# Routing up to the slots ahead of the experts, the data-dependent branch behind them, and the first weight splits on VectorE: one decoder layer on one core

## The chip, the core and the metric

The kernel runs on one core of a Trainium2 chip. The core has five engines with an instruction stream each: TensorE (PE, with the loading of its weights shown apart as PEld), VectorE (DVE), ScalarE (ACT), GpSimd (POOL) and SyncE (SP), and 16 DMA engines that serve the queues of SP and POOL. An engine works its own stream in the order in which it is written and waits on semaphores for the others. The metric is the device time of one execution in microseconds (us). Lower is better.

## The reference

One layer of a decoder for 576 tokens: 512 of a prompt and 64 of a sample (8 sequences of 8). Everything is fp32, with a model width of 1024.

```
proj   = rmsnorm(x) @ w_in                  # 1024 x 5632
y_a    = differential attention(...)        # prompt: causal; sample: a paged cache of 4096
y_r    = HGRN2 gated linear recurrence(...)
merged = sigmoid(gate_a)*(y_a @ w_branch_a) + sigmoid(gate_r)*(y_r @ w_branch_r)
x      = x + merged @ w_out
h      = rmsnorm(x)
group  = top 1 of 4 (h @ w_rg + b);  experts = top 2 of the 4 in that group (h @ w_re + b)
x      = x + sum of 2 of  w * (silu(h @ w_gate[e]) * (h @ w_up[e])) @ w_down[e]     # 16 experts, width 256
x      = x + sigmoid(rmsnorm(x) @ w_ple_gate) * (p @ w_ple)                          # per-layer input
y      = rmsnorm(x)
```

## The kernel before

**Precision.** Products run in fp32r. A weight arrives as a raw fp32 tile and is taken apart in two parts, `hi` (a cast on ACT) and `lo` (raw minus hi, a subtraction on DVE or POOL), and a product is three products of parts.

**Lanes.** The program is written by lanes, Python generators that a small scheduler (`run_lanes`) interleaves while the kernel is built: it keeps an estimate of each engine's clock and takes, of the lanes whose event is set and whose buffers are free, the one of the best priority. What comes out is one fixed stream per engine. All instructions are issued through one helper, so nearly every row of the trace has its line, L209 (L207 after the change); places are told by the tiles' names. Buffers are pools of slots that lanes take and give back.

**Stages.** Input projection, attention and recurrence, the branches and the output projection (`out_second`, products into `acc`, `sc`, `aux`), with the router's logits of each of the five tiles of tokens behind them (`lane_route`; it also stores the normed rows h to memory, `hf_d<-F`). Then comes `lane_dispatch`, a chain of small operations, mostly DVE's, on all tokens at once. It finds each token's group and two experts (`oh`, as bf16 `mb`), counts places with five small products (`aux<-mb,cbf`), and gathers with one-hot products (`rhs`, `am`) the **slots**: for each expert the tokens of its tile of 128 rows. Behind the slots it works out what the later stages need: the number of tiles beyond one per expert (`cnt`, `nov`, `ovb`, `ge`, `ovx`), the slots of those further tiles (`r`, `aux<-r,am`), the place of each token's two results (`rows`) and their weights (`wt`).

**The gap.** Between the last product of the output projection and the first of the experts, PE has only the small products of the dispatch and those of the per-layer input (`ple_mul`, `in<-mr,rp` and `sc<-mr,rp`). Meanwhile the first NG=5 pieces of the experts' weights are split (`lane_msplit`: hi on ACT, lo on POOL), and POOL gathers the rows of the first tiles (`X<-hf_d,slots`).

**The branch.** Before the experts stands `further()`: seven nested `If`s on the number of tiles beyond the 17 that are always worked. With this data none is taken, but every engine has to load the number and jump past the bodies. Its code is there because other data could need it.

```
for j in range(1, MAXOV):
    si.enter_context(tc.If(nov > j))
```

**Experts.** `lane_moe` works 17 tiles: 16 experts, and one further tile. A tile takes 6 pieces of weights of 512 KB (`mload` to slots `mr`, `mro`, `H`; `wsplit` to `mw`, `mwo`), the gathered rows `X` turned on PE (`sc<-constb,X`) and split (`xs`), four groups of products `in<-mw,xs`, the activation `hd`, its turn `sc<-constb,hd`, its split `hs`, and the second product `aux<-mw,hs` / `acc<-mw,hs`, copied to `Yo` and stored (`y_d<-Yo`).

**Tail.** `lane_tail` does the last three `ple_mul`, gathers each token's two results (`mr<-y_d,rows`), adds them (`H<-mr,wt,H`), turns the rows (`sc<-constb,H`), and does the per-layer gate's products and the last norm.

Of the kernel before, what the change touches and what calls it, by code (L numbers as in the profile page):

```python
# [27 lines left out]
H = 4  # L28
# [14 lines left out]
def _consts():  # L43
    """Tables that depend on the shapes alone."""
# [61 lines left out]
PT = ("X", "Xo", "mro")  # L106
NPE = 2
PEV = 9
NMW = 10
NY = 3  # L110
YT = "Yo",
MPACE = 98, 1
HYS = 4, 7
NMX = 0
NX = 2
# [3 lines left out]
PLO = []  # L119
# [19 lines left out]
# the weights' chunks in the order of their use  # L139
# [45 lines left out]
class Engine:  # L185
    """Passes instructions on and keeps an estimate of the engine's clock, by which the lanes are interleaved."""
# [62 lines left out]
class Kern:  # L249
# [16 lines left out]
    # ------------------------------------------------ lanes  # L266
# [39 lines left out]
    def pick(self, *tags, n=1):  # L306
        """Which of several tags has n slots free: one that ends in o is for the further tiles until they are through."""
        def f():
            for t in tags:
                if (t[-1] == "o" if self.inner else t[-1] != "o" or self.fev.t is not None):  # L310
                    if self.used.get(t, 0) + n <= self.cap.get(t, 0) - (0 if self.gapev.t is None else self.mres if t == "mr" else self.hres if t == "H" else 0):
                        return t
            return None
        return f
# [12 lines left out]
    def pool(self, st, name, tags, **kw):  # L327
        """A pool with a number of slots per tag, counted as the lanes take and free them."""
# [26 lines left out]
    def aside(self, f):  # L355
        """Runs f without making the lane wait for what it issues; returns the time it ends."""
# [9 lines left out]
    def rstd(self, ss, n, shape):  # L366
        """(ss / n + EPS) ** -0.5 by Newton's steps from the exponent's estimate."""
# [23 lines left out]
    # ---------------------------------------------------------------- start  # L391
# [19 lines left out]
    def setup_rest(self):  # L411
        nc, a = self.nc, self.a
        # lambda, on every partition
# [12 lines left out]
        # 1 for the first map's rows, -lambda for the second's  # L426
# [5 lines left out]
        # lower bound of the forget gate: f = fa + fb * tanh(z / 2)  # L432
# [22 lines left out]
    def lane_start(self):  # L455
        """x * g_mix in two parts, and the norm's factor per token along the free dimension."""
# [128 lines left out]
    def in_proj(self, i):  # L585
        """One tile of 128 columns of the input projection, for all tokens, with the norm's factor."""
# [68 lines left out]
    def lane_gates(self):  # L655
        """The branches' gates, back from memory."""
# [12 lines left out]
    def to_tok(self, z, tok, tail):  # L669
        """[128, 576] to the token-major [128, 4, 128] and [64, 128]."""  # L670
# [11 lines left out]
    def rope(self, x, c0, c1, sh):  # L682
        """Rotates x ([128, ...] with the positions c0..c1 last) in place."""
# [58 lines left out]
    def lane_attn(self):  # L742
        """Scores and weights of the prompt's attention, by head and block of queries."""
# [38 lines left out]
    def lane_mid(self, waits, st):  # L782
        """When the first phase's lanes are through, their space goes to the next phase's inputs."""
# [13 lines left out]
    # ------------------------------------------------ sample: the new tokens  # L797
# [35 lines left out]
    # ------------------------------------------------ sample: the paged cache  # L833
# [18 lines left out]
    def lane_scores(self):  # L852
        """Scores of 8 pages at a time by (head, page of a pair, token, map), their maxima, weights and sums."""
# [164 lines left out]
    # ---------------------------------------------------------------- branches, output projection  # L1018
# [14 lines left out]
    def branches(self):  # L1033
# [4 lines left out]
        for b in (1, 0):  # L1038
            for m in range(8):
# [21 lines left out]
                if b == 0:  # L1061
# [3 lines left out]
                    def merge():  # L1065
                        nc.gpsimd.tensor_tensor(g, g, gr, op=ALU.add)
# [9 lines left out]
    def rows_setup(self):  # L1076
        """Constants and weights of the routing."""
# [31 lines left out]
    def lane_route(self, i):  # L1109
        """The router's logits of a tile of tokens; its rows with the norm's weights, and behind them what belongs to the norm itself."""  # L1110
        nc = self.nc
        t0, n = TOK[i]
        for j in range(2):
# [11 lines left out]
            def store():  # L1125
                nc.gpsimd.tensor_tensor(hg[:n], xs, self.grow[0][:n, j * 512:j * 512 + 512], op=ALU.mult)
# [40 lines left out]
    # ---------------------------------------------------------------- routing  # L1167
# [3 lines left out]
    # ---------------------------------------------------------------- experts  # L1171
# [16 lines left out]
    def lane_msplit(self, keys):  # L1188
        """The first tiles' weights, while the routing is under way."""
        yield self.gapev  # L1190
        for key in keys:
            yield from self.wsplit(key, True)

    def lane_mx(self, tiles):
        """The tokens' rows of each tile."""
# [3 lines left out]
        for tl in tiles:  # L1199
            if tl == NE:  # L1200
                yield self.slev2
            w = self.pick("X", "Xo")
            yield w
            tag = self.xt[tl] = w()
            x = self.tl(tag, [128, D + 2])
# [1007 lines left out]
```

## Time and profile before

| | before |
|---|---|
| device time, median of 3 runs | 1026.29 us |
| the three runs | 1024.25, 1030.06, 1026.29 us |
| span of the profiled execution | 1028.9 us |
| PE / PEld busy | 957.8 us (93%) / 766.8 us (75%) |
| DVE busy | 675.4 us (66%) |
| ACT busy | 433.4 us (42%) |
| POOL busy | 344.0 us (33%) |

For the profiled execution the trace gives its span, first to last instruction on the core; that is the time against which the rows below add up. It lies among the three runs, 2.6 us above their median. Times inside the span count from its start: the projections, attention and recurrence take the first 727 us, the gap runs from there to some 767, the experts to 944 and the tail to the end. Busy shares are means over all of it.

### The profile page before, as it was taken

The numbers are of one execution on the slowest core, as the hardware profiler recorded it, in microseconds if no ns is written. First come the engines' busy times: TensorE is split into PE (matmuls) and PEld (weight loads), VectorE is DVE, ScalarE is ACT, GpSimd is POOL, SyncE is SP. The second block draws the span as 40 slices with busy tenths as digits, with TensorE's granted clock in tenths as the row PEclk, the third lists the DMA queues.
The fourth block names the chain that finished last, engine by engine and source line by source line (L and its number), as shares of the span: only waits on it lengthen the run. The fifth ranks groups of instructions, "written<-read, shape, count | busy, mean of one in ns | idle before, by whom it ended". The sixth has DMA issues, their size and how long they took to land. (4 is left out here: it accounts for less than half of the span.)

```text
span 1028.9 us, 20982 instructions
## 1 busy us (share of the span) xinstructions
PE 957.8 (93%) x8129; PEld 766.8 (75%) x8129; DVE 675.4 (66%) x1701; ACT 433.4 (42%) x875; POOL 344.0 (33%) x370
## 2 busy tenths in 40 slices
PE   6999999999999999999999989989639999998995
PEld 5986787877877878778878879868427777775683
DVE  6554555567866774864764465433778999996775
ACT  5143544353342323123222232232228888886442
POOL 3125545454455453543463111332340110101200
PEclk9999999999999999999999989999869999998998
DMA  7549989998989898897997437854149999993511
GB/s 235 206 154 406 367 304 341 313 299 287 335 306 344 311 333 284 297 348 240 332 342 289 139 106 264 291 195 179 46 158 326 393 413 411 412 413 136 186 42 51
DMA packets 93066, 278.67 MB, mean 271 GB/s; under 512 B 10288, under 2 KB 15168, under 8 KB 92960
## 3 DMA queue, kind: packets, MB, share of 16 engines
q0 software_dynamic: 42880, 155.28, 42.5%
q1 hardware_dynamic: 48496, 118.73, 31.7%
q10 hardware_dynamic: 1584, 3.24, 0.8%
q8 instruction: 67, 1.10, 0.4%
q14 instruction: 39, 0.32, 0.1%
HBM read 251.95 MB, written 25.27 MB: 269 GB/s over the span
## 5 line engine op out<-in xcount | busy, mean ns | idle before, releaser
L209 PE MATMUL in<-H,hi 128*128 128x288 f32 x1592 | 357.0, 315 | 14.1 <-ACT hi L209 5.9
L209 PEld LDWEIGHTS in<-H,hi 128*128 128x128 f32 x1592 | 258.9, 193 | 52.1 <-issue 31.3
L209 PE MATMUL in<-H,lo 128*128 128x288 f32 x796 | 239.1, 300 | 0.5 <-DVE lo L209 0.5
L209 POOL DMA_INDIRECT V<-in_vc,idxv x128 | 127.8, 998 | 192.1 <-PE acc L209 172.7
L209 POOL DMA_INDIRECT K<-in_kc,idxk x128 | 126.4, 987 | 104.9 <-PE sc L209 58.1
L209 PEld LDWEIGHTS in<-H,lo 128*128 128x128 f32 x796 | 153.2, 193 | 1.5 <-DVE lo L209 1.2
L209 PE MATMUL in<-mw,xs 128*128 128x512 f32 (+1 forms) x462 | 119.3, 405 | 0.0
L209 DVE TENSOR_TENSOR lo<-raw,hi 128x512 fp32r<-128x512 f32 x116 | 79.7, 691 | 49.5 <-ACT hi L209 48.2
L209 ACT CAST hi<-raw 128x512 fp32r<-128x512 f32 x116 | 70.1, 616 | 84.8 <-PE in L209 58.7
L209 PEld LDWEIGHTS in<-mw,xs 128*128 128x128 f32 (+1 forms) x462 | 85.3, 190 | 20.2 <-DVE xs L209 0.3
L209 PE MATMUL acc<-V,ptz 128*32 128x128 f32 x2048 | 80.8, 277 | 2.1 <-DMA V<-in_vc,idxv 2.0
L209 ACT COPY F<-aux 128x512 f32<-128x512 f32 (+3 forms) x74 | 30.0, 405 | 115.5 <-PE aux L209 115.4
L209 DVE TENSOR_TENSOR mw<-mr,mw 128x1024 fp32r<-128x1024 f32 x58 | 69.2, 1220 | 3.4 <-ACT mw L209 3.4
L209 PEld LDWEIGHTS acc<-V,ptz 128*32 128x32 f32 x2048 | 51.8, 109 | 24.0 <-issue 16.0
L209 PE MATMUL sc<-K,qbd 128*32 128x256 f32 x1024 | 68.9, 387 | 0.7 <-DMA K<-in_kc,idxk 0.7
L209 ACT CAST mw<-mr 128x1024 fp32r<-128x1024 f32 x63 | 65.0, 1056 | 9.0 <-DMA hf_d<-F 7.1
L209 POOL DMA_INDIRECT X<-hf_d,slots x16 | 15.4, 964 | 109.7 <-DVE mw L209 106.0
L209 PE MATMUL aux<-F,F 128*128 128x128 f32 (+6 forms) x216 | 48.0, 394 | 0.2 <-ACT F L209 0.2
L209 DVE TENSOR_TENSOR F<-in,rb 128x288 f32<-128x288 f32 x62 | 27.9, 451 | 29.7 <-PE in L209 29.5
L209 PEld LDWEIGHTS sc<-K,qbd 128*32 128x32 f32 x1024 | 28.3, 110 | 24.0 <-issue 9.3
L209 ACT ACTIVATE F<-F 128x576 f32<-128x576 f32 (+1 forms) x33 | 22.4, 680 | 51.1 <-POOL F L209 26.4
L209 PE MATMUL aux<-mw,hs 128*128 128x512 f32 x150 | 41.8, 415 | 0.5 <-ACT hs L209 0.5
(399 smaller groups left out, 1549.6 us busy)
## 6 DMA issues: line engine op xcount, KB each, us to landing
mr<-in_w_gu SPq DMA_DIRECT2D x55, 512.0 KB, 8.6
raw<-in_w_in SPq DMA_DIRECT2D x88, 256.0 KB, 5.0
mr<-in_w_dn SPq DMA_DIRECT2D x22, 512.0 KB, 10.4
y_d<-Yo SPq DMA_DIRECT2D x17, 512.0 KB, 11.4
raw<-in_w_br SPq DMA_DIRECT2D x16, 256.0 KB, 2.9
raw<-in_w_out SPq DMA_DIRECT2D x16, 256.0 KB, 5.8
H<-in_w_gu SPq DMA_DIRECT2D x7, 512.0 KB, 8.7
y_d<-G SPq DMA_DIRECT2D x1, 3584.0 KB
```

What stands on the lines that cost most here:

```text
L209: return f(*a, **kw)
```

## The change

1. The dispatch runs only as far as the slots. The experts' lane starts with the others, and what follows the slots in the dispatch waits for the event `x0ev`, set behind the turning of the first tile's rows. The activation `hd` of a tile waits for the end of the dispatch (`dispev`).
2. `further()` moves from ahead of the experts to behind them: behind the 17 tiles and the last `ple_mul`, ahead of the gathers of the tail. Its bodies use slots of other pools.
3. Work leaves POOL: the 5 lo splits in the gap go to DVE (three behind the slots, two more behind `x0ev`), their 5 hi casts on ACT stand in a row; the 8 merges of the two branches (128x576) and the 10 products `hg` of `lane_route` (128x512) go to DVE.
4. Idle products on PE, which nothing reads: 3 of 128x128 by 512 columns in fp32 behind the counting products, and 4 behind the slots (`warm`).
5. Slots: `mw` 10 to 12 and `X` 2 to 3 in place of `mwo`, `Xo`, `mx`, which existed apart for the further tiles.

```
@@ out_second
-                        nc.gpsimd.tensor_tensor(g, g, gr, op=ALU.add)
+                        nc.vector.tensor_tensor(g, g, gr, op=ALU.add)
@@ lane_route
-                nc.gpsimd.tensor_tensor(hg[:n], xs, self.grow[0][:n, j * 512:j * 512 + 512], op=ALU.mult)
+                nc.vector.tensor_tensor(hg[:n], xs, self.grow[0][:n, j * 512:j * 512 + 512], op=ALU.mult)
@@ lane_msplit
         yield self.gapev
         for key in keys:
-            yield from self.wsplit(key, True)
+            yield from self.wtake(key)
+            self.aside(lambda: nc.scalar.copy(self.mw[key][0], self.mraw[key][0]))
+        yield self.slev
+        for i, key in enumerate(keys):
+            if i == 3:
+                yield self.x0ev
+            hi, lo = self.mw[key]
+            raw, tag = self.mraw[key]
+            self.aside(lambda: nc.vector.tensor_tensor(lo, raw, hi.bitcast(F32), op=ALU.subtract))
...
@@ run
-            self.run_lanes(alls + self.xgev[:1])
+            moe = self.spawn(self.lane_moe(tiles, HORDER[NG:]), 1)
+            self.spawn(self.lane_rest(moe), 0)
+            self.run_lanes()
             self.further()
-            for l in self.lanes:
-                l.prio = min(l.prio, 1)
-            moe = self.spawn(self.lane_moe(tiles, HORDER), 1)
-            self.spawn(self.lane_tail(moe), 0)
+            self.spawn(self.lane_tail(), 0)
             self.run_lanes()
@@ lane_dispatch
+        self.warm(NWARM[0])
...
         self.set(self.slev)
+        self.warm(NWARM[1])
+        yield self.x0ev
@@ warm
+            p = self.tl("acc", [128, 512])
+            for _ in range(n):
+                self.nc.tensor.matmul(p, self.ones, self.constb[:, :512], start=True, stop=True)
@@ lane_moe
+            if t == 0 and g and not self.inner:
+                self.set(self.x0ev)
...
         def act(t):
+            yield self.dispev
```

The order of the streams shows what the diff does not. The first place is DVE's stream behind the slots: `z` to `ovx` are the count of further tiles, `xs` the split of an expert tile's turned rows, `mw` the lo split of a weight piece. Before:

```order
L209 COPY lo_8939<-aux_8925 128x16
L209 SCALAR_TENSOR_TENSOR slots_8938<-aux_8925,lo_8939 128x16
L209 MEMSET z_1448_8959 128x16
L209 COPY cnt_8955<-aux_8949 128x16
L209 TENSOR_SCALAR nov_8956<-cnt_8955 128x16
L209 SCALAR_TENSOR_TENSOR nov_8956<-cnt_8955,nov_8956 128x16 x3
L209 SCALAR_TENSOR_TENSOR inc_8957<-z_1448_8959,nov_8956 128x16
L209 TENSOR_TENSOR ovb_8958<-inc_8957,nov_8956 128x16
L209 TENSOR_TENSOR ge_8971<-ovb_8958,constb_115 128x128
```

After the change:

```order
L207 SCALAR_TENSOR_TENSOR slots_8945<-aux_8932,lo_8946 128x16
L207 TENSOR_TENSOR mw_8904<-mr_7957,mw_8903 128x1024
L207 TENSOR_TENSOR mw_8907<-mr_7969,mw_8906 128x1024
L207 TENSOR_TENSOR mw_8910<-mr_7982,mw_8909 128x1024
L207 TENSOR_TENSOR xs_8979<-sc_8980,xs_8979 128x512
L207 TENSOR_TENSOR xs_8979<-sc_8987,xs_8979 128x512
L207 TENSOR_TENSOR mw_8913<-mr_7991,mw_8912 128x1024
L207 TENSOR_TENSOR mw_8916<-mr_8086,mw_8915 128x1024
L207 TENSOR_TENSOR mw_9005<-mr_8112,mw_9004 128x1024
L207 TENSOR_TENSOR mw_9018<-mr_8114,mw_9017 128x1024
L207 TENSOR_TENSOR xs_9029<-sc_9030,xs_9029 128x512
L207 TENSOR_TENSOR mw_9038<-mr_8144,mw_9037 128x1024
```

Two more `mw` follow, and then `MEMSET z`, `COPY cnt` and the rest of the dispatch to `wt`, and behind it the first tile's `hd`. So 10 splits and three `xs` now stand between the slots and the count of further tiles, where none stood; before, 5 of these splits were POOL's and 5 stood on DVE behind the branch.

The second place is PE's stream around the branch (`ovx` is the number of further tiles; `X` and `Xo` in its bodies are rows of further tiles). Before, behind the last small products of the dispatch:

```order
L209 MATMUL aux_9001<-r_1461_8993,am_8919 128x16
L1829 TENSOR_LOAD ovx_8987
L1830 COMPARE_AND_BRANCH
L209 MATMUL sc_9079<-constb_115,Xo_9076 128x128 x4
L209 MATMUL sc_9086<-constb_115,Xo_9076 128x128 x4
L209 MATMUL in_9101<-mwo_9095,xs_9078 128x512
```

After the change, behind the last `ple_mul` (`in<-mr,H`) of the tail:

```order
L207 MATMUL in_10914<-mr_7833,H_9547 64x512
L207 MATMUL in_10917<-mr_7832,H_9547 64x512
L207 MATMUL in_10917<-mr_7833,H_9547 64x512
L1847 TENSOR_LOAD ovx_9096
L1848 COMPARE_AND_BRANCH
L207 MATMUL sc_10955<-constb_115,X_10952 128x128 x4
L207 MATMUL sc_10962<-constb_115,X_10952 128x128 x4
```

The branch now has the last products of the per-layer input ahead of it and the turning of the tail's rows behind it. On DVE, ACT, POOL and SP it moves likewise from the gap to the tail.

## Rows read from the trace of the kernel before

**Rows 1.** Windows: length, busy us of PE, PEld, DVE, ACT, POOL, clock, DMA share, GB/s.

```profile
740.00:750.00 10.00, 6.59 (x28) 2.91 (x27) 8.23 (x17) 3.16 (x6) 5.02 (x3) 0.70 0.01 2
750.00:760.00 10.00, 0.44 (x10) 0.34 (x10) 8.99 (x21) 1.91 (x3) 5.95 (x4) 0.64 0.62 210
...
825.00:925.00 100.00, 96.38 (x462) 76.48 (x461) 94.53 (x111) 86.30 (x121) 10.42 (x19) 1.00 1.03 412
```

**Rows 2.** The chain that ended last, two tiles apart: start, length, engine and tile.

```profile
904.29 2.35 DVE mw L209 x2
...
914.29 2.35 DVE mw L209 x2
```

**Rows 3.** PE's timeline in the gap: start, us, operation, form, count, [idle before <-releaser].

```profile
742.07 4.74 PE L209 MATMUL sc<-mr,rp 128*128 128x512 f32 x6
...
759.44 0.44 PE L209 MATMUL aux<-r,am 128*128 128x16 bf16 x10 [9.94 <-DVE r L209]
...
765.07 1.94 PE L209 MATMUL sc<-constb,X 128*128 128x128 f32 x8 [5.19 <-ACT mw L209]
...
777.89 0.41 PE L209 MATMUL sc<-constb,hd 128*128 128x128 f32 x2 [1.58 <-issue]
```

**Rows 4.** DVE's timeline in the gap, same columns.

```profile
739.70 2.11 DVE L209 TENSOR_TENSOR mb<-oh 128x80 bf16<-128x80 f32 x1
...
744.07 2.32 DVE L209 TENSOR_SCALAR rhs<-ohq,constc 128x160 bf16<-128x160 f32 x1
...
746.32 0.31 DVE L209 TENSOR_TENSOR rhs<-ohq,tidx 128x160 bf16<-128x160 f32 x1
...
748.69 0.17 DVE L209 SCALAR_TENSOR_TENSOR slots<-aux,lo 128x16 int32<-128x16 f32 x1
...
751.25 2.34 DVE L209 TENSOR_TENSOR ge<-ovb,constb 128x128 f32<-128x128 f32 x1
...
754.14 3.01 DVE L209 TENSOR_TENSOR ge<-ge,constb 128x128 f32<-128x128 f32 x1
...
762.97 0.17 DVE L209 TENSOR_TENSOR wt<-wt,d 128x5 f32<-128x5 f32 x1
```

**Rows 5.** POOL's timeline in the gap.

```profile
739.28 2.43 POOL L209 TENSOR_TENSOR mw<-mr,mw 128x1024 fp32r<-128x1024 f32 x1 [3.10 <-ACT mw L209]
...
749.15 1.02 POOL L209 DMA_INDIRECT X<-hf_d,slots  x1 [2.86 <-DVE z L209]
```

**Rows 6.** DMA issues from 740 to 800 us: count, KB each, median us to landing.

```profile
mr<-in_w_gu SPq DMA_DIRECT2D x11, 512.0 KB, 4.3
...
X<-hf_d,slots POOLq DMA_INDIRECT x5, 6.9
```

**Rows 7.** The page's groups: DVE's lo split (busy us, mean ns, idle before).

```profile
L209 DVE TENSOR_TENSOR mw<-mr,mw 128x1024 fp32r<-128x1024 f32 x58 | 69.2, 1220 | 3.4 <-ACT mw L209 3.4
```

**Rows 8.** The page's groups: POOL's gathers of the experts' rows.

```profile
L209 POOL DMA_INDIRECT X<-hf_d,slots x16 | 15.4, 964 | 109.7 <-DVE mw L209 106.0
```

**Rows 9.** SP's timeline, the next loads of weights.

```profile
753.46 3.88 SPq L209 DMA_DIRECT2D mr<-in_w_gu  x2
```

**Rows 10.** The instructions of line 1830, the branch: ns min/median/max, first and last start.

```profile
L1830 PEldq COMPARE_BRANCH  x1: 3642/3642/3642, 760.1 to 760.1; - x1
...
L1830 DVEq COMPARE_BRANCH  x1: 72/72/72, 763.6 to 763.6; - x1
```

**Rows 11.** PE's timeline at the tail's start.

```profile
950.87 3.65 PE L209 MATMUL in<-mr,H 128*64 128x512 f32 x8
...
955.75 0.63 PE L209 MATMUL sc<-constb,H 128*128 128x128 f32 x4 [1.24 <-DVE H L209]
```

**Rows 12.** Timelines of DVE, POOL and PE in the output projection.

```profile
683.98 0.68 DVE L209 TENSOR_TENSOR H<-H,aux 128x512 f32<-128x512 f32 x1
...
682.99 1.60 POOL L209 TENSOR_TENSOR F<-H,H 128x512 f32<-128x512 f32 x1 [13.34 <-DVE H L209]
...
684.71 1.11 PE L209 MATMUL aux<-constb,H 128*128 128x128 f32 x4 [2.61 <-DVE H L209]
```

More of the change, by code (lines that the diff above doesn't have):

```diff
@@ L105 @@
 NE2 = 1
-PT = ("X", "Xo", "mro")
+PT = ("mr", "mr", "H")
 NPE = 2
 PEV = 9
-NMW = 10
+NMW = 12
 NY = 3
-YT = "Yo",
 MPACE = 98, 1
 HYS = 4, 7
-NMX = 0
-NX = 2
+NX = 3
+NWARM = 3, 4
 SWITCH = 0.0
@@ L118 @@
 PA, PB = 0.066, 2050
-PLO = []
 STEP = "satsbxsmcssdsnhy"
@@ L309, in f @@
             for t in tags:
-                if (t[-1] == "o" if self.inner else t[-1] != "o" or self.fev.t is not None):
-                    if self.used.get(t, 0) + n <= self.cap.get(t, 0) - (0 if self.gapev.t is None else self.mres if t == "mr" else self.hres if t == "H" else 0):
-                        return t
+                r = 0 if self.gapev.t is None else self.mres if t == "mr" else self.hres if t == "H" else 0
+                if self.used.get(t, 0) + n <= self.cap.get(t, 0) - r:
+                    return t
             return None
@@ L1188, in lane_msplit @@
     def lane_msplit(self, keys):
+        nc = self.nc
         yield self.gapev
         for key in keys:
-            yield from self.wsplit(key, True)
+            yield from self.wtake(key)
[7 more added lines that the diff above has]
+            self.aside(lambda: nc.vector.tensor_tensor(lo, raw, hi.bitcast(F32), op=ALU.subtract))
+            self.free(tag)
+            self.set(self.mwev[key])
+            yield
     def lane_mx(self, tiles):
@@ L1666, in lane_dispatch, with warm, f @@
         self.set(self.dispev)
+    def warm(self, n):
+        def f():
+            p = self.tl("acc", [128, 512])
+            for _ in range(n):
+                self.nc.tensor.matmul(p, self.ones, self.constb[:, :512], start=True, stop=True)
+            self.free("acc")
+        self.aside(f)
     def mload(self, key):
@@ L1671, in mload @@
         pg = key[0] == "pg"
-        w = self.pick(*(("mr", "mro") if pg else ("H", "mr", "mx", "mro") if self.gapev.t is not None else ("mr", "H")))
+        w = self.pick(*(("mr",) if pg else ("mro",) if self.inner else ("H", "mr", "mro") if self.gapev.t is not None else ("mr", "H")))
         yield w
@@ L1697, in lane_tail @@
         self.free("mr", 2)
-        k = min(10, NMR - 2 - max(0, 14 - NMW - NMX))
-        yield ("mr", k)
-        yield ("mro", 1)
-        yield ("X", 10 - k)
-        rt = ["mr"] * k + ["X"] * (10 - k)
+    def lane_tail(self):
+        nc = self.nc
+        room = {t: self.cap[t] - self.used[t] for t in ("mr", "mro", "X", "mw")}
+        rt = [t for t in room for _ in range(room[t])][:10]
+        yield None
         ys, ss, xs, ps, r2 = [], [], {}, {}, {}
@@ L1987, in lane_gap, with wtake, wroom, wsplit @@
         self.ca.close()
-        self.pool(self.ctx, "pXg", {"X": NX, "Xo": 1, "mro": 2})
-        self.pool(self.ctx, "pM", {"mw": NMW, "mwo": 2, "mx": NMX, "xs": 2})
+        self.pool(self.ctx, "pXg", {"X": NX, "mro": 2})
+        self.pool(self.ctx, "pM", {"mw": NMW, "xs": 2})
         self.set(self.gapev)
-    def wsplit(self, key, pool=False):
-        nc = self.nc
+    def wtake(self, key):
         yield self.mrev[key]
-        pg = key[0] == "pg"
-        w = self.pick("mw", "mwo", *(("mx", "mr") if pg else ()), n=2)
+        w = self.wroom(key)
         yield w
         tag = self.mwt[key] = w()
-        hi, lo = self.mw[key] = [self.tl(tag, [128, 1024], F32R) for _ in range(2)]
+        self.mw[key] = [self.tl(tag, [128, 1024], F32R) for _ in range(2)]
+    def wroom(self, key):
+        return self.pick("Yo" if self.inner else "mw", *(("mr",) if key[0] == "pg" else ()), n=2)
+    def wsplit(self, key):
+        nc = self.nc
+        yield from self.wtake(key)
+        hi, lo = self.mw[key]
         raw, tag = self.mraw[key]
         def split():
-            if pg:
+            if key[0] == "pg":
                 g = self.smalls[:, SM["g_ple"][0] + key[1]:][:, 0:1]
@@ L2008, in split @@
             else:
-                nc.scalar.copy(hi, raw)
-                (nc.gpsimd if pool else nc.vector).tensor_tensor(lo, raw, hi.bitcast(F32), op=ALU.subtract)
-        if self.dispev.t is None:
-            split()
-        else:
-            self.aside(split)
+                self.split(hi, lo, raw)
+        self.aside(split)
         self.free(tag)
@@ L2021, in lane_moe @@
         nt = len(tiles)
-        todo = [k for k in keys if k not in self.mw]
-        xs, xr, ps, hid, hs, y, yt, count = {}, {}, {}, {}, {}, {}, {}, [0]
+        todo = list(keys)
+        xs, xr, ps, hid, hs, y = {}, {}, {}, {}, {}, {}
         def sp():
-            if todo and self.mrev[todo[0]].t is not None and self.pick("mw", "mwo", *(("mx", "mr") if todo[0][0] == "pg" else ()), n=2)() is not None:
-                count[0] += 1
-                yield from self.wsplit(todo.pop(0), count[0] % 6 in PLO)
+            if todo and self.mrev[todo[0]].t is not None and self.wroom(todo[0])() is not None:
+                yield from self.wsplit(todo.pop(0))
         def need(key):
@@ L2057, in mt @@
                 self.aside(lambda: nc.gpsimd.tensor_copy(xr[t], self.xg[tl][:, D:]))
-                self.free(self.xt[tl])
+                self.free("X")
         def gu(t, q):
@@ L2124, in dn @@
                 self.aside(lambda: nc.sync.dma_start(self.y_d[tl * 128:tl * 128 + 128, :], y[t]))
-                self.free(yt.pop(t))
+                self.free("Yo")
         ops = {"a": lambda t: gu(t, 0), "b": lambda t: gu(t, 1), "c": lambda t: gu(t, 2), "d": lambda t: gu(t, 3),
```

27 lines of the change are left out of this document (11 added, 16 removed).

## The prediction

> **What bounds the kernel now.** I read the stages first [rows 1]. From 825 to 925 us PE (96%) and DVE (95%) are both full and the DMA engines are too; from 740 to 760 nobody carries the time: PE has 7.0 us of work in 20, the DMA engines stand nearly still for half of it, and PE's granted clock falls to 0.70 and 0.64 of full speed, a mixture of its two levels, 1.2 and 2.4 GHz. So there are two regimes: a loop of the experts that is limited by engines, and a gap ahead of it that is limited by a chain.
>
> The chain of waits shows the loop [rows 2]: the same DVE splits end it at 904.29 and at 914.29, and between them come only PE and DVE, each released by the other. One tile costs 10.0 us. What the gap gains therefore arrives at the end of the experts only as far as the first tile's activation `hd` comes earlier; what is done earlier inside the gap, but not on the way to that `hd`, is lost.
>
> PE's own stream [rows 3] gives the gap's shape. Products of 512 columns take some 0.8 us each at 742 (4.74 us for 6, the slow level), the further tiles' products come at 759.44 after 9.94 us of idleness, the first rows are turned at 765.07, and the first `hd` is turned at 777.89, which is the mark that I follow. DVE's stream [rows 4] shows what PE waits for: a dispatch of operations of 0.2 to 0.3 us, broken by four of 2.1 to 3.0 us. Their sizes don't explain that: `rhs<-ohq,constc` takes 2.32 us and its twin of the same shape, `rhs<-ohq,tidx`, 0.31. POOL's stream [rows 5] does: in each of the four a lo split of POOL's runs (2.43 us the one at 739.28, beside `mb` at 739.70; three more of that kind stand beside the others).
>
> **The change part by part.**
>
> *Splits leave POOL.* The four operations fall back to their twin's 0.3 us. `mb` gives 1.8 us and `rhs` 2.0 ahead of the slots; the two `ge` give 2.0 and 2.7 behind them. Ahead of the slots I take 3.1 of the 3.8, because three idle products (0.8 us each at the slow level, as in [rows 3]) now stand on PE between the counting products and the slots', and can hold them up. The slots then end at 748.69 + 0.17 - 3.1 = 745.8.
>
> *First tile.* The gather of its rows is issued 0.3 us after the slots in [rows 5] (749.15), so now at 746.1; gathers here take 6.9 us to land (median of five) [rows 6], so 753.0. PE has four idle products and four of the per-layer input ahead of the turning, 8 x 0.85 from 745.6 = 752.4, so it is ready. So the turning starts at 753.0 in place of 765.07, 12 us earlier. That number is the tempting one; it is not the gain.
>
> *DVE takes the path.* Its stream now has, behind the slots, 3 splits, 2 `xs`, 4 splits, 1 `xs`, 3 splits, the rest of the dispatch, and only then `hd`. A split is 1.22 us [rows 7], `xs` 0.7. From 745.8: 3.7 gives 749.5; idle to the first `xs`, 1.0 behind the first turning, at 754.1; 1.4 + 4.9 + 0.7 + 3.7 gives 764.8. The rest of the dispatch took 763.14 - 748.86 = 14.3 us [rows 4]; less 4.7 of stalls and some 0.6 of waits for products that are now done early, 9.0. So it ends at 773.8, `hd` takes 1.0, and it is turned at 774.8 in place of 777.89: **-3.1 us**. The 6 us of splits that DVE takes over from POOL are in this sum, and they are why 12 us shrink to 3. Bounds: if the rows land after 4.3 us, as the weights of the same stretch do [rows 6], DVE idles 2.6 less, and with the slots 3.8 and not 3.1 earlier something near -5 is left. If two of them come late, or PE, asleep from 759 to 769, does its next products at the slow level (0.85 in place of 0.41 for 6 or so): -1.
>
> A rule of the Trainium skill speaks against this part ("SBUF — State Buffer", Who interferes with whom): a DVE operation with two SBUF inputs and a GpSimd instruction that reads SBUF shut each other out for a whole instruction. The gather reads its slots from SBUF and is now issued into three such splits; by that rule it could start up to 3 x 1.22 = 3.7 us late, and -3.1 would become about 0. In the trace the 16 gathers, most of them beside such splits, last 0.96 us in the mean, not longer than the 1.02 of the one in the idle gap [rows 5, 8]; I go by the rows.
>
> *Earlier loads.* SP's next loads of weights went out at 753.46 behind a split of POOL's [rows 9]; now a slot comes free at 747, and the DMA engines start 6.5 us earlier. The loop is not theirs (above), so I count nothing; that is a rival.
>
> *The branch.* In the gap PE's jump is one record of 3642 ns; on DVE it is 72 ns [rows 10]. In the gap that cost goes away, which the sum above holds already (no jump stands in DVE's new way to `hd`). In the tail it comes back. There PE ends its last per-layer product at 950.87 + 3.65 = 954.5 and is released by DVE to turn rows at 955.75, after 1.24 us [rows 11]. With the jump between the two: 954.5 + 0.2 for loading the number + 3.64 + 0.1 = 958.45, **+2.7**. From below: if the jump were as short as DVE's, PE would still be held by the gathers, which stand behind SP's and POOL's own jumps: 0. From above: the whole idle stretch around the jump in the gap, 5.19 us [rows 3], gives 959.7, +3.9. I take **+3.0**, nearer the record. DVE's, ACT's and POOL's jumps end while the gathers travel, and cost nothing as long as that cover holds.
>
> The Trainium skill gives about 108 ns for a compare-and-branch ("Advanced Engine Details and Errata", Control Flow Timing); DVE's row agrees and PE's is 34 times that. By that figure the tail would pay nothing, 3 us less. Another page has the reason why a jump may be long ("Runtime: NRT & Kernel Launch", Instruction fetch mechanics): a taken branch to code that is not yet near must fetch it first. No row here tells fetching from jumping.
>
> *Merges and `hg` on DVE.* One `hg` is 128x512, as `H<-H,aux` is, 0.68 us on DVE [rows 12]. POOL's took 1.60 and nobody waited for it. On DVE one stands ahead of the sum `H<-H,aux` of the third tile of tokens and two ahead of the fourth's; PE idles 2.61 us for the first of these sums (684.71, the bank `aux`). 1 to 3 of them exposed make +0.7 to +2.0; the merges are faster on DVE and may give 0.5 back. I take **+1.0**, with -0.5 to +2.5.
>
> *Slots of `mw` and `X`.* The number of `mw` is the same 12, and the per-tile order of the loop's instructions is too; nothing. The idle products cost PE only time in which it idled.
>
> **Sum.** -3.1 + 3.0 + 1.0 = +0.9 us: 1028.9 to 1029.8 in the profiled execution, which lies 2.6 us above the median of the three runs. Against that median, 1026.29, it is 1027.2. Taking 0.5% (5.1 us) as what a measurement of this kernel tells from no change, this is no change. With the bounds of the three terms (-5 to -1, 0 to +3.9, -0.5 to +2.5) the likeliest case runs from 1021 to 1032.
>
> **Rivals.**
>
> *The jump in the tail is hidden* (PE's stream runs ahead while its last 8 products, 3.65 us, still work). For it: DVE's 72 ns. Against: in the gap PE stood idle right through the record. The tail costs 0.3 or so: -3.1 + 0.3 + 1.0 = -1.8, 1024.5. Still within 0.5%.
>
> *The loads set the experts' pace*, and the earlier restart is kept. For it: DMA share 1.03 at 412 GB/s in [rows 1]. Against: the chain of [rows 2] passes through no DMA there. If all 6.5 us are kept, and the first 12 us earlier products let PE and DVE follow, the gap gives between 6.5 and 12: 1026.3 + 4.0 - 9 = 1021, faster by about 0.5%, down to 1018.
>
> *DVE becomes the bound in the gap* (the other side). The stream is in order: one late piece of weights or one late gather in front of the count of further tiles delays the rest of the dispatch, and with it `wt`, `hd` and every tile behind. Pieces six to ten are loaded only when splits free their slots, from 747 on, and compete with three gathers. If DVE reaches the count at 769 in place of 764.8, `hd` is turned at 779, +1.1, and with tail and front +5.1: 1031.4. From there on it is slower; at 771 it is 1033.5.
>
> **How the numbers follow.** Chances: my sum 0.45, jump hidden 0.12, loads' pace 0.22, DVE late 0.21. Faster by over 0.5% takes 0.15 of the loads' case and 0.10 from the low ends of the first two: 0.25. Slower takes most of DVE's case, 0.17, and 0.05 from the sum's high end: 0.22. Same: 0.53. I forecast 1027 us; the range, with no more than 2 in 10 left out, is 1018 to 1033, the first reaching to the loads' case and the second to DVE's.
>
> **What would show it.** In the changed kernel's trace: no operation of 2 us among the dispatch's small ones, and slots at about 746; the first `in<-mw,xs` near 755 but the first `sc<-constb,hd` near 775; tiles still 10.0 us apart; a jump of PE's of 3 to 4 us after the last `in<-mr,H`, and the first `sc<-constb,H` some 4 us behind that product. I am wrong if the tiles come closer together than 10.0, if `hd` moves by more than 5 us either way, or if the tail's turning follows the products without a pause.

## The result: slower by 0.6%, and how the profile after looks

| | before | after |
|---|---|---|
| median of 20 runs each | 1029.28 us | 1034.41 us |
| lowest and highest | 1021.90, 1036.12 us | 1030.47, 1044.89 us |
| ratio after to before, 95% interval | | 1.0063 (1.0037 to 1.0089) |
| span of the profiled execution | 1028.9 us | 1029.5 us |

The forecast was 1027 us, no change, and a range up to 1033. It set out from the median of three runs, 1026.29 us; the median of twenty is 1029.28, so 3.0 of the 7.4 us between forecast and time belong to that starting value, and the change itself makes +5.1 us (0.5%) between the medians. Ratios, here and below, are over the fast runs, which leaves out single runs more than 1.5% above the fastest of their kernel. The two profiles alone would have borne it out, with +0.6 us. They are not typical: the execution profiled after took 1031.32 us, 3 us less than the median of its kind, and executions of either kernel differ by over 10 us. So this section reads the pair, and the experiments ask which of the stages differ from one profile to the next.

DVE's timeline of the changed kernel in the gap answers to [rows 4]:

```profile
739.93 0.24 DVE L207 TENSOR_TENSOR mb<-oh 128x80 bf16<-128x80 f32 x1
...
742.44 0.30 DVE L207 TENSOR_SCALAR rhs<-ohq,constc 128x160 bf16<-128x160 f32 x1
...
746.24 0.17 DVE L207 SCALAR_TENSOR_TENSOR slots<-aux,lo 128x16 int32<-128x16 f32 x1
746.64 3.50 DVE L207 TENSOR_TENSOR mw<-mr,mw 128x1024 fp32r<-128x1024 f32 x3 [0.23 <-issue]
755.72 1.29 DVE L207 TENSOR_TENSOR xs<-sc,xs 128x512 fp32r<-128x512 f32 x2 [5.58 <-ACT xs L207]
...
766.95 0.29 DVE L207 TENSOR_TENSOR ge<-ovb,constb 128x128 f32<-128x128 f32 x1
...
773.90 0.17 DVE L207 TENSOR_TENSOR wt<-wt,d 128x5 f32<-128x5 f32 x1
```

The four long operations are gone, each now 0.2 to 0.3 us, and the slots are there 2.5 us earlier. Behind them stands what the order showed: three splits, 5.58 us of waiting for the first turned rows, the other splits, and the rest of the dispatch, which ends at 774.07 (763.14 before).

PE's timeline in the same place answers to [rows 3]:

```profile
754.43 1.06 PE L207 MATMUL sc<-constb,X 128*128 128x128 f32 x8 [1.48 <-DMA mro<-in_w_gu]
...
770.39 0.41 PE L207 MATMUL aux<-r,am 128*128 128x16 bf16 x10 [8.02 <-DVE r L207]
...
776.05 0.66 PE L207 MATMUL sc<-constb,hd 128*128 128x128 f32 x2 [1.74 <-ACT xs L207]
776.36 2.91 PE L207 MATMUL in<-mw,xs 128*128 128x512 f32 x6
...
787.67 0.41 PE L207 MATMUL sc<-constb,hd 128*128 128x128 f32 x2 [0.37 <-DVE hd L207]
```

The first rows are turned 10.6 us earlier (754.43 for 765.07), the first `hd` only 1.8 us (776.05 for 777.89), and the second stands 11.6 us behind it instead of 10.0: of the gap's gain 0.2 us is left one tile on. The six products behind the first `hd` take 2.91 us; at the full clock six of the kind take 1.64. The windows of the changed kernel (columns as in [rows 1]) show the clock there:

```profile
750.00:760.00 10.00, 8.28 (x34) 5.05 (x33) 4.42 (x6) 4.91 (x9) 4.03 (x5) 1.00 0.96 334
760.00:770.00 10.00, 2.37 (x15) 1.72 (x14) 9.48 (x27) 3.03 (x4) 0.00 (x0) 0.80 0.95 365
770.00:780.00 10.00, 7.87 (x33) 6.06 (x33) 6.09 (x22) 2.62 (x7) 1.13 (x2) 0.52 0.20 59
```

While DVE works the rest of the dispatch (9.48 us busy in ten) PE idles for 8 us, and then works at 0.52 of full speed, nearly all of it at 1.2 GHz. Before, the slow stretch lay at 754 to 769 us and was over ahead of the first `hd`.

At the tail, the instructions of the branch's line (it is line 1848 now), PE's timeline, and POOL's first gather:

```profile
L1848 SPq EVENT_SEMAPHORE  x9: 17/17/17, 945.8 to 948.3; - x9
...
L1848 SPq COMPARE_BRANCH  x1: 50/50/50, 942.9 to 942.9; - x1
...
L1848 PEldq COMPARE_BRANCH  x1: 3911/3911/3911, 946.6 to 946.6; - x1
L1848 DVEq EVENT_SEMAPHORE  x1: 21/21/21, 948.7 to 948.7; - x1
```

```profile
947.95 3.65 PE L207 MATMUL in<-mr,H 128*64 128x512 f32 x8
957.09 1.09 PE L207 MATMUL sc<-constb,H 128*128 128x128 f32 x4 [5.49 <-DVE H L207]
```

```profile
949.12 0.95 POOL L207 DMA_INDIRECT mr<-y_d,rows  x1 [31.42 <-DVEq L1848]
```

PE's jump is as long as it was in [rows 10], but it starts at 946.6, while PE's products run on to 951.6: its stream is read ahead of its work, and the jump is covered. SP's is not. Its compare is at 942.9, right behind the last store of results, its nine semaphores are raised from 945.8 to 948.3, and the gathers, which read those results, come at 949.12. PE waits 5.49 us for them, where it waited 1.24 [rows 11]. The gather's row names DVE's semaphore of the same line, at 948.7, because that one came last; whether the gather waited for it or for SP's is what an experiment below decides.

### The profile page after: what moved, and what is told of

It is laid out like the page before. It is cut to its first block, busy times and chain, and to the rows that moved or that the text cites. A ratio compares the mean times of both kernels' runs of the same rounds, so it can differ in the third digit from the quotient of the medians.

```text
span 1029.5 us, 21005 instructions
## 1 busy us (share of the span) xinstructions
PE 960.6 (93%) x8143; PEld 766.7 (74%) x8143; DVE 680.5 (66%) x1724; ACT 433.7 (42%) x875; POOL 314.6 (31%) x347
## 5 line engine op out<-in xcount | busy, mean ns | idle before, releaser
L207 PE MATMUL in<-mw,xs 128*128 128x512 f32 (+1 forms) x588 | 152.8, 405 | 0.2 <-ACT xs L207 0.2
L207 PEld LDWEIGHTS in<-mw,xs 128*128 128x128 f32 (+1 forms) x588 | 107.4, 189 | 24.8 <-ACT xs L207 0.5
L207 DVE TENSOR_TENSOR mw<-mr,mw 128x1024 fp32r<-128x1024 f32 x77 | 92.0, 1222 | 4.6 <-ACT mw L207 4.2
L207 ACT CAST mw<-mr 128x1024 fp32r<-128x1024 f32 x77 | 79.3, 1054 | 4.5 <-DVE lg L207 4.1
L207 PE MATMUL aux<-F,F 128*128 128x128 f32 (+6 forms) x216 | 47.7, 391 | 0.2 <-ACT F L207 0.2
L207 POOL DMA_INDIRECT X<-hf_d,slots x17 | 22.9, 1345 | 77.0 <-DVE mw L207 45.9
L207 ACT ACTIVATE F<-F 128x576 f32<-128x576 f32 (+1 forms) x33 | 22.4, 680 | 48.9 <-DVE F L207 48.9
L207 DVE TENSOR_TENSOR F<-F,F 128x576 f32<-128x576 f32 (+3 forms) x49 | 32.8, 684 | 15.5 <-ACT F L207 14.8
## 6 DMA issues: line engine op xcount, KB each, us to landing
y_d<-Yo SPq DMA_DIRECT2D x17, 512.0 KB, 11.5
```

Of the source, the lines that this page charges most:

```text
L207: return f(*a, **kw)
```

## The experiments

The accounts that the expectations name: A, three small terms and a profiled execution that happened to be quick; B, the merges and `hg` on DVE cost 3 to 5 us in most executions (B', it is the merges); C, the tail's jump varies; D and E, it is the kernel before that varies, by GpSimd's splits or by its branch; F, `hg` leaves PE at its slow level in the output projection. Kernels that were timed together ran on one chip, in turn with the kernel before. The level differs from set to set (median of before 1029 to 1031 us in some, 1066 to 1069 in others); the difference lies ahead of the output projection, which starts at 641 to 647 us or at 678 to 684. So only ratios and the lengths of stages compare across sets.

The stages in us, from the rows of each profile: **front** from the first `acc<-hi,F` of the output projection to the last `acc<-Hy,F`; **gap** from there to the first `sc<-constb,hd`; **experts** to the last; **tail** to the end of the span. **Gather** is the first gather of results, counted from the start of the last `in<-mr,H`.

| kernel | front | gap | experts | tail | gather | ratio to before |
|---|---|---|---|---|---|---|
| before | 86.6 | 49.2 | 159.8 | 91.2 | -5.8 | |
| before_1 | 86.2 | 49.6 | 159.7 | 90.9 | -5.9 | |
| before_2 | 88.0 | 48.9 | 159.6 | 87.5 | -5.7 | |
| after | 87.8 | 46.9 | 161.3 | 92.2 | -1.9 | 1.0063 |
| again | 96.5 | 45.9 | 159.7 | 95.2 | -2.1 | 1.0035 (1.0014 to 1.0057) |
| again_2 | 96.6 | 45.9 | 159.8 | 95.4 | -1.8 | 1.0040 (1.0006 to 1.0074) |
| b_front_dve | 87.9 | 49.3 | 159.6 | 90.1 | -6.1 | 1.0011 (0.9979 to 1.0042) |
| a_front_pool | 86.8 | 47.8 | 161.2 | 92.4 | -1.7 | 1.0030 (1.0010 to 1.0050) |
| a_merge_pool | 87.9 | 46.4 | 161.2 | 93.3 | -1.8 | 1.0051 (1.0012 to 1.0090) |
| a_hg_pool | 87.5 | 49.9 | 159.5 | 93.5 | -1.8 | 1.0024 (0.9997 to 1.0051) |
| a_nobranch | 87.8 | 46.8 | 161.1 | 87.2 | -5.7 | 1.0027 (0.9995 to 1.0060) |
| a_front_pool_nobranch | 84.1 | 49.8 | 161.1 | 88.4 | -5.8 | 0.9983 (0.9954 to 1.0013) |
| b_nobranch | 87.4 | 47.7 | 159.5 | 90.3 | -5.9 | 0.9976 (0.9956 to 0.9996) |
| a_store_pool | 87.6 | 48.0 | 161.2 | 90.6 | -5.1 | 1.0018 (0.9989 to 1.0046) |
| b_split_dve | 87.9 | 49.0 | 159.7 | 91.1 | -5.9 | 0.9971 (0.9953 to 0.9988) |
| b_split_dve_2 | 86.6 | 49.1 | 159.7 | 91.4 | -6.2 | 1.0012 (0.9978 to 1.0046) |
| a_nowarm | 87.7 | 46.2 | 161.1 | 93.6 | -1.9 | 1.0032 (1.0010 to 1.0055) |
| a_warm8 | 90.3 | 46.2 | 162.4 | 93.5 | -1.8 | 1.0091 (1.0057 to 1.0125) |
| a_store_warm8 | 87.4 | 47.7 | 161.0 | 88.5 | -5.1 | 0.9998 (0.9971 to 1.0025) |
| a_store_warm8_3 | 86.7 | 47.9 | 159.6 | 92.2 | -5.0 | 0.9994 (0.9964 to 1.0025) |

**The two kernels again (again, again_2, before_1, before_2).** No edit.

> The changed kernel once more, for a second profile. In the one profile the marks moved so: end of the unchanged part at 588 us -1.0, last product of the output projection +0.4, slots -2.5, first turned hd -1.8, last turned hd -0.3, first product of the tail +1.7, end +0.6; the timed runs moved by +5. Theory A (three small terms: front +1.4, experts -0.6, tail +1.7, together 2 to 3, and the profiled execution was a quick one): the same differences between the marks, the time +3 to +6 over before. Theory B (merges and hg on DVE cost more in most executions): the distance from 588 to the last product of the output projection is 3 to 5 us longer than before's in this profile. Theory C (the jump in the tail varies): the distance from the last ple_mul to the tail's first product is 3 to 6 us longer than in the first profile.

> The changed kernel unchanged, for the same rounds: +0.4 to +0.7% against before, and 5 to 8 us above a_store_warm8_3 if both causes hold; 3 to 5 if only the tail's does.

> The kernel before, unchanged, for a second profile. Its timed runs spread over 12 us without a tail, those of the changed kernel with its front on GpSimd over 4 us, so something in it varies. Theory D (the gap of before varies: where GpSimd's splits fall beside DVE's operations differs from one execution to the next): the stretch from the last product of the output projection to the first turned hd, 49.2 us in the first profile, comes out shorter by 3 to 8 us when the time is low. Theory E (the jump ahead of the experts varies): the stretch from wt to the first turned hd, 14.9 us, is what changes. Theory A (nothing varies there): all stretches behind 640 us within 0.5 us of the first profile.

> The same kernel a third time, with the same expectations as for the second profile; two profiles with different spans tell D, E and A apart better than one.

The changed kernel was slower each time, by 0.35% and 0.40%, and both profiles have a stage that the first did not show: the front takes 96.5 us, 9 us more. PE's wait in it is 2.93 us, hardly longer than before's 2.61 [rows 12]. The windows of again (columns as in [rows 1]) show what there is instead, and PE's timeline that wait and a short one behind it:

```profile
730.00:740.00 10.00, 8.99 (x35) 7.15 (x33) 2.02 (x5) 2.41 (x6) 1.09 (x2) 0.50 0.15 54
740.00:750.00 10.00, 10.00 (x36) 8.25 (x36) 3.61 (x8) 2.62 (x6) 1.10 (x2) 0.50 0.49 160
750.00:760.00 10.00, 10.00 (x49) 8.00 (x49) 2.11 (x4) 1.14 (x2) 0.00 (x0) 0.97 0.73 273
```

```profile
727.35 1.11 PE L207 MATMUL aux<-constb,H 128*128 128x128 f32 x4 [2.93 <-DVE H L207]
...
734.71 1.12 PE L207 MATMUL aux<-constb,H 128*128 128x128 f32 x4 [0.73 <-ACT F L207]
```

PE is busy nearly all through and works at 0.50 of full speed for 24 us. Before, the slow level lasts 3 to 7 us at this place. Three profiles speak against D and E: the kernel before has nearly the same gap in each (48.9 to 49.6). What varies in it is the tail, 87.5 or 91: PE idles 2.3 us ahead of the last `hd` in both, and falls to the slow level behind it in some executions and not in others. The products behind the last `hd` in before and in before_2:

```profile
938.62 2.93 PE L209 MATMUL aux<-mw,hs 128*128 128x512 f32 x6 [0.52 <-ACT hs L209]
```

```profile
939.81 1.67 PE L209 MATMUL aux<-mw,hs 128*128 128x512 f32 x6 [0.52 <-ACT hs L209]
```

**The front (b_front_dve, a_front_pool, a_hg_pool, a_merge_pool).** The two lines of the diff, set in the kernel before, undone together, and undone apart:

```
 merge   nc.gpsimd | nc.vector .tensor_tensor(g, g, gr, op=ALU.add)
 hg      nc.gpsimd | nc.vector .tensor_tensor(hg[:n], xs, self.grow[0]...)
```

> The kernel before with the 8 merges and 10 hg products on DVE, nothing else. Theory A: +1.4 us (0.14%) over before, all between 640 and 730 us. Theory B: +4 us or more (0.4%). Theory C: within 0.15% of before.

> The changed kernel with the 8 merges and the 10 hg products back on GpSimd, nothing else. Theory A: 1.4 us less than the changed kernel, the stretch from 588 us to the last product of the output projection as before the change; against before +2 to +4 (0.2 to 0.4%). Theory B: 4 us or more less, the time of before within 0.2%. Theory C: no change, +0.5 to 0.6% over before.

> The changed kernel with the 10 hg products alone back on GpSimd (the merges stay on DVE). So far 17 of 56 timed runs of kernels with both on DVE lie 8 to 14 us above their other runs, and none of 114 with both on GpSimd; in the one such profile PE's clock stays at its slow level for 24 us in the output projection instead of 3 to 7. Theory F (two hg ahead of the fourth tile's sum leave PE idle for another 0.73 us while it is at the slow level, and in some executions it stays there): no run lies 7 us above the median here, and the wait of 0.73 us for F is gone; against before +0.2 to +0.4%. Theory B' (it is the merges): 3 to 5 of 12 runs lie high.

> The changed kernel with the 8 merges alone back on GpSimd (hg stays on DVE). Theory F: 2 to 5 of 12 runs lie 8 to 14 us above the others, the wait of 0.73 us for F is there; against before +0.4 to +0.6%. Theory B': no high run.

The wait of 0.73 us for F is in every profile with `hg` on DVE, a_merge_pool among them, and in none with it on GpSimd; that part of F is shown. Front stages: with `hg` on DVE 8 profiles, two of 96.5, one of 90.3, five of 87.7 to 87.9, mean 90.3; with it on GpSimd 12 profiles, 84.1 to 88.0, mean 86.9. That is +3.4 us on the mean, +1 mostly and +9 now and then.

The granted clock tells the two kinds apart. With `hg` on GpSimd the slow stretch in the front lasts 3 to 4 us in five profiles and about 7 in six, and one has none. With `hg` on DVE it lasts 3 to 4 us in five, and is over before the short wait. In the other three (a_warm8, again, again_2) the short wait falls into it, and it lasts 10, 24 and 24 us. So F holds as far as the profiles go, three against six; why the level comes back early in some executions is open.

The timed runs bear it out for the two lines together. Runs more than 7 us above their kernel's median: 13 of 98 with `hg` on DVE, 1 of 107 in the edited kernels with it on GpSimd, and 5 of 164 of the kernel before. (By this rule the 56 runs that the expectation of a_hg_pool speaks of give 9, not 17.) They don't part `hg` from the merges: a_merge_pool has one such run of 10, a_hg_pool one of 11, another 6.9 us above, and a run of 2306 us, unlike any other and left out. The profiled execution of a_hg_pool is one of the two, with a normal front, 4 us lost ahead of it and 2 in the gap; high runs have more than one cause.

In the kernel before the two lines cost 5.1 us on the mean of the twelve runs of b_front_dve and 2.9 between the medians; its ratio, 1.0011, leaves out its three highest runs, 1081 to 1084 us. Undone in the changed kernel they give back little: a_front_pool is 0.3 us below again between the medians, 1.4 on the mean. The table shows why: with `hg` back on GpSimd the front is shorter and the changed gap longer, 47.8 to 49.9 (a_front_pool, a_hg_pool, a_front_pool_nobranch, a_store_pool) for 45.9 to 46.9 (after, again, again_2, a_merge_pool, a_nobranch, a_nowarm). What links `hg` to the gap was not tested.

**The tail (a_nobranch, a_front_pool_nobranch, b_nobranch, a_store_pool).** The first three leave out the branch's bodies, which this data doesn't run (b_nobranch besides moves on the scheduler's estimates of the clocks); the last keeps them and changes a queue:

```
-            self.further()
+            pass
@@ a_store_pool (with merges and hg on GpSimd)
-                self.aside(lambda: nc.sync.dma_start(self.y_d[tl * 128:tl * 128 + 128, :], y[t]))
+                q = nc.gpsimd if self.inner else nc.sync
+                self.aside(lambda: q.dma_start(self.y_d[tl * 128:tl * 128 + 128, :], y[t]))
```

> The changed kernel without the branch over further tiles in the tail (its seven bodies are left out; with this data none of them runs). Theory A: the gathers of the tail go out some 1 to 2 us earlier and the time falls by 1.7 us, to about +0.3 to 0.4% over before. Theory B: falls by 1 to 2 as well. Theory C: falls by 4 to 6, to the time of before.

> The changed kernel with merges and hg on GpSimd and without the branch in the tail (its bodies left out; none runs with this data). If the loss is the tail's jump and the long slow phase and nothing else, this is 4 us faster than the changed kernel with its front on GpSimd (which was +0.30% over before): -0.1 to -0.3% against before, with no high runs, and last turned hd to end 87 to 88 us. If something else in the changed kernel costs time that no profile has shown, it stays at +0.1% or more.

> The kernel before without the branch over further tiles (its bodies are left out; none runs with this data). Theory A: the path to the first hd loses the stretch of PE's jump, 3 to 5 us, and the time falls by 0.3 to 0.5%. Theory E: falls by more, 6 us on the mean, and the spread of its runs shrinks from 12 to about 5 us. Theory D: falls by 3 to 5 and the spread stays 12.

> The changed kernel with merges and hg on GpSimd, and the stores of the branch's bodies on GpSimd's queue instead of SP's; the branch stays in the tail. The gathers then need no semaphore that SP raises behind its jump. If SP's jump is what the tail waits for: the first gather comes 5.7 us ahead of the last per-layer product's start, as in the kernels without the branch, not 1.9; the tail is 3 to 4 us shorter and the time -0.1 to -0.3% against before. If PE's jump is: first products of the tail as late as now, no gain, about +0.3%.

The column of the gathers parts the kernels cleanly: -5.7 to -6.2 us without a branch in the tail, -1.7 to -2.1 with it. So the branch costs the gathers some 3.9 us, each time. a_store_pool tells whose jump it is. PE's jump is there and as long as ever (3771 ns), and the gathers are back at -5.1: they go out before SP has raised its last semaphore, and 2.6 us before DVE raises the one that the changed kernel's row names. So neither PE's jump nor DVE's semaphore held them, but SP's path. Its branch line's semaphores, its first gather, and PE's first turning:

```profile
L1848 SPq EVENT_SEMAPHORE  x9: 17/17/103, 984.2 to 984.9; - x9
...
L1848 DVEq EVENT_SEMAPHORE  x1: 21/21/21, 987.0 to 987.0; - x1
```

```profile
984.43 1.52 POOL L207 DMA_INDIRECT mr<-y_d,rows  x1 [28.26 <-SPq L1848]
```

```profile
992.44 1.09 PE L207 MATMUL sc<-constb,H 128*128 128x128 f32 x4 [2.38 <-DVE H L207]
```

PE's wait for the first turned rows is 5.0 to 5.5 us in the eight profiles with the branch in the tail, 2.4 to 2.5 in the three with that edit, and 0.9 to 1.7 in the others; what the remaining 1.2 us are was not looked into. The tail is 90.4 us on the mean of the three, 93.6 on the mean of the eight, and 90.4 on the mean of six with the branch in the gap; single tails differ by 4 us with the level behind the last `hd`. The runs alone don't show the gain of this one edit: a_store_pool's 1.0018 and a_front_pool's 1.0030 have overlapping intervals, and a_store_pool was expected below 1. The ratio of a_nobranch (1.0027) is higher than its stages give; its median is 1069.32 beside 1073.39 for again, timed together, and four of its twelve runs lie 6 to 12 us above it, as runs with `hg` on DVE do. b_nobranch, without the branch in the gap, gains 0.24%, a little under theory A's 0.3 to 0.5%, with a gap 1.5 us shorter.

**The gap (b_split_dve twice, a_nowarm, a_warm8, a_store_warm8, a_store_warm8_3).** The five splits alone moved in the kernel before; the idle products taken out; more of them put where PE idles:

```
@@ b_split_dve
-            yield from self.wsplit(key, True)
+            yield from self.wsplit(key)
@@ a_nowarm
-NWARM = 3, 4
+NWARM = 0, 0
@@ a_warm8, behind the products pn (a_store_warm8: with the edits of a_store_pool)
+        self.warm(8)
@@ a_store_warm8_3, besides, in act
             yield self.dispev
+            if t == 0 and not self.inner:
+                self.warm(3)
```

> The kernel before with the five lo splits of the gap on DVE, at their places in the order (three of them ahead of the slots), nothing else. Theory A: the four long operations shrink to 0.3 us and five splits of 1.2 us come in: slots about where they were, the rest of the dispatch 2 us shorter, the time -2 to 0. Theory D: the spread of the runs shrinks to about 5 us and the time rises, to +2 to +4, since the low runs of before are gone. Theory E: spread as before.

> The kernel before with the lo splits of the gap on DVE, once more. If its lead (0.9971) was real: -0.15 to -0.45% against before again. If it was a draw of quick runs: within 0.1%.

> The changed kernel without the 7 idle products. If they only fill time in which PE waits: within 0.1% of the changed kernel, and slots up to 0.7 us earlier since nothing stands ahead of the slots' products. If they hold the clock up: PE turns the first rows at the slow level, the first turned hd comes 0.5 to 1.5 us later. If they delay the slots by more: first turned hd up to 1 us earlier.

> The changed kernel with 8 more idle products on PE, 7.4 us at the full clock, behind the products that count the further tiles, where PE now idles for 8 us. If PE's slow clock is what stretches the first tiles: the distance from the first to the last turned hd is 159.6 us again, not 161.2, the first turned hd comes 0.5 to 1 us earlier, and the time falls by 1.5 to 2.5 us (0.15 to 0.25%). If the two tiles are held up by DVE's order: no change.

> Both: stores of the bodies, merges and hg on GpSimd, and the 8 more idle products. If both causes hold: 5 to 6 us less than the changed kernel, -0.2 to -0.5% against before. If only the tail's: as a_store_pool.

> As a_store_warm8, with three more idle products (2.8 us) ahead of the last turning before the first hd. If the slow clock behind the first hd is what costs 1.6 us: the second hd is turned 10.0 us behind the first, first to last 159.7 us, and the time 1.5 us below a_store_warm8's, -0.2% against before. If the clock is not the cause, the distance stays 11.5.

The splits alone leave the gap of the kernel before as it was (49.0, 49.1). The idle products of the change are worth nothing measurable: the gap is 46.2 us without them and 45.9 to 46.9 with them. My eight more did not help either: a_warm8, against its expectation, is slower still (1.0091, over eight runs, experts 162.4), and a_store_warm8 (0.9998) lies within the interval of a_store_pool. PE's timeline of a_store_warm8 shows a reason: PE now works from 804 to 813.5, then waits 3.41 us for the first `hd`, and falls to the slow level just there.

```profile
816.88 0.66 PE L207 MATMUL sc<-constb,hd 128*128 128x128 f32 x2 [3.41 <-ACT xs L207]
817.19 2.91 PE L207 MATMUL in<-mw,xs 128*128 128x512 f32 x6
```

With three more ahead of that wait, in a_store_warm8_3, the clock holds:

```profile
809.38 2.82 PE L207 MATMUL acc<-constb,ones 128*128 128x512 f32 x6
...
814.77 0.41 PE L207 MATMUL sc<-constb,hd 128*128 128x128 f32 x2 [0.75 <-ACT xs L207]
814.93 1.65 PE L207 MATMUL in<-mw,xs 128*128 128x512 f32 x6
...
824.77 0.41 PE L207 MATMUL sc<-constb,hd 128*128 128x128 f32 x2 [0.37 <-DVE hd L207]
```

Six products take 1.65 us, the second `hd` is turned 10.0 us behind the first, and the experts take 159.6 us as before the change. That the slow clock behind the first `hd` costs 1.6 us is shown by all profiles together: the two `hd` stand 9.97 to 10.0 us apart where the products between them run at the full clock, and 11.5 to 12.8 where they don't. That the three idle products hold the clock is one profile, and again, again_2 and a_hg_pool stand 10.0 apart without them. a_store_warm8_3 ends level with the kernel before (0.9994), 0.5% below the changed kernel timed with it (1.0040), by all its edits together. b_split_dve looked like the version that beats both (0.9971), but not when run again (1.0012).

## Why the prediction was wrong

By its own steps:

*Splits leave POOL*: right. The slots end at 746.41 against 745.8 forecast.

*First tile* and *DVE takes the path*: the place of the bound was right, and nearly the size. DVE's stream did set the first `hd`: -2.8 us on the mean of the six profiles with this gap and `hg` on DVE (46.4 for 49.2), where -3.1 stood. Of these 2.8 the slow clock behind the first `hd` takes back 1.0 on the mean of the same six (experts 160.7 for 159.7), 1.6 where it falls. I had it as the lower bound, "its next products at the slow level", at 1 to 2 us, and took the value without it. So this term is **-1.8, not -3.1**. I had set aside a rule of the Trainium skill ("SBUF — State Buffer", Who interferes with whom): a GpSimd instruction that reads SBUF and a DVE operation with two SBUF inputs shut each other out. It may have a part here: the first gather now goes out 0.95 us behind the slots and lasts 1.38 us, where it went out 0.3 behind and lasted 1.02 [rows 5], and the next one 1.93. That is about 1 us, not the 3.7 that the rule would allow. The two gathers of the changed kernel in POOL's timeline:

```profile
747.36 1.38 POOL L207 DMA_INDIRECT X<-hf_d,slots  x1 [10.95 <-DVE slots L207]
749.04 1.93 POOL L207 DMA_INDIRECT X<-hf_d,slots  x1 [0.30 <-issue]
```

*The branch*: +3.0 forecast, **+3.2** measured (93.6 for 90.4). The number came out by luck, for the path was wrong. I priced PE's jump as exposed; it is covered by PE's own queue of products, as the rival had it. What I named as cover, the gathers "behind SP's and POOL's own jumps", and put at 0, is the cost. The rival's sum, 0.3 for the tail, left that out too.

*Merges and `hg` on DVE*: **the step that failed most**. +1.0 forecast, +3.4 on the mean of the profiles. One to three `hg` exposed at their length is what most profiles show (+1). What the sum had no term for is the clock: where PE is still at its slow level when the added wait comes, the level lasts 10 to 24 us in place of 7. The 3.4 leans on two profiled executions that were the highest and the second highest of twelve. If the long stretch comes as often as the high runs do, 13 in 98, the term is about +2 (an estimate from these counts and the fronts of the table).

Together -1.8 + 3.2 + 3.4 = +4.8 us, or some +3.5 with that estimate, beside +5.1, +4.2 and +3.7 between the medians of the three sets in which the changed kernel was timed; the forecast was +0.9. So the part that failed twice is PE's clock: no term for it in the front, and a bound that was named and not taken behind the first `hd`. The chance for slower, 0.22, hung on another mechanism, DVE late in the gap, which did not happen (the count of further tiles is reached at 765.5, forecast 764.8). The rival of the loads' pace is out as well: loads restart at 748 and the tiles behind the second stay 10.0 us apart. None of the signs that the prediction gave for being wrong appeared; none of them looked at the front.

What stays open: why the slow level in the front ends after 3 to 4 us in some executions and not in others with nearly the same first wait, and why PE's jump takes 3.6 to 3.9 us. The Trainium skill gives 108 ns for a compare-and-branch ("Advanced Engine Details and Errata", Control Flow Timing). The trace has 50 ns for SP, below that, and 3911 for PE, 36 times as long. But SP's short record is followed by 2.9 us to its first semaphore and 2.5 us of raising them, and that is what the tail paid.

## What to carry to other kernels

When a data-dependent branch moves, follow for each engine what is raised behind its jump and who waits for it; the queue that issues the stores can cost more than the engine with the longest jump. A small operation put ahead of one that PE waits for can cost more than its length where PE is at its slow level: here the same 0.73 us of waiting went with 1 us lost in some executions and 9 in others. Where PE already idles, price the slow level behind it too. And two profiles decide nothing below one per cent when executions differ by as much: compare stages over several.

## What I had not expected of the hardware

PE stayed at the slow level for 24 us with a busy share of 90 to 100% (again, 730 to 750 us); I had taken slow stretches to end within 3 to 7 us, as they do at this place in all profiles of before. And the same idle time of 2.3 us ahead of the last `hd` is followed by the slow level in some executions (before, tail 91.2 us) and not in others (before_2, 87.5 us).
